# Gate and up projections: two of three matmul passes joined into one, and two sums of weights made by adding transfers

## The chip, the cores and the metric

One core of a Trainium2 chip runs the whole program. The metric is device time in microseconds (us) of one execution, as the median of several. Beside it there is one profiled execution with a trace of every instruction; all durations below are from that one. The engines are PE (matmuls; its weight loads stand apart as PEld), DVE (elementwise work), ACT (copies, casts, activations), POOL and SP. In the part of the program that is changed, SP and POOL only issue transfers (DMA). Each engine works through its own list of instructions in a fixed order, and an instruction that waits holds up all behind it on the same engine.

## The reference

One layer of an encoder on 512 tokens of width 2048, all in float32: a mixer, cross-attention into 256 memory tokens, and a SwiGLU feed-forward part, each between two norms. The change lies in the first half of the feed-forward part, the gate and up projections:

```python
def swiglu_ffn(h, w_gu, w_down):          # h: 512 x 2048, w_gu: 2048 x (5632 gate | 5632 up)
    gate, up = jnp.split(h @ w_gu, 2, axis=-1)
    return (jax.nn.silu(gate) * up) @ w_down
...
x = x + rmsnorm(swiglu_ffn(rmsnorm(x, g[FFN_PRE]), ffn_w_gu[l], ffn_w_down[l]), g[FFN_POST])
```

## The kernel before, in words

The program runs `phase1` (mixer), `phase2` (attention), `gate_up`, `down` and `last`, one after the other. `gate_up` is the stage from about 1440 us to 2330 us of the span.

`gate_up` works through 44 blocks `j` of 128 hidden columns. A block multiplies the 512 tokens by 2048 x 256 weights (128 gate columns and 128 up columns). It is cut into halves three ways: tokens into two halves of 256, the inner dimension into two halves of 1024, columns into gate and up. The 2x2 block product is formed by seven half-size products instead of eight, a scheme of Strassen's kind: each product multiplies a sum of quarters of the activations (`L[1]` to `L[7]`, made once, kept in SBUF) by a sum of quarters of the weights. In the order in which a block runs them, the products are 1, 2, 6, 5, 7, 3, 4. The text calls them P1, P2, P6 and so on.

The four quarters of the weights of a block are `w_gu[j, kh, g]`, 128 x 1024 numbers or 512 KB each: B11 (`kh` 0, gate), B12 (0, up), B21 (1, gate), B22 (1, up). P1, P2 and P3 take B11, B21 and B22 as they are. The other four take sums: S5 = B11 + B12, S6 = S5 + B22, S7 = B12 + B22, S4 = S6 + B21. Before, DVE makes all four (lines 1027, 1030, 1032, 1034 in `right_parts`).

A float32 factor is split into a high and a low part (`split3`): ACT casts the high part (`whi`, line 988), DVE subtracts to get the low part (`wlo`, line 989). A product then runs, for each of 8 inner tiles `k`, three matmuls of 128 weights columns by 256 tokens (`mul3`, lines 177 to 179): high by high, high by low, low by high, all summed into one PSUM bank half. So a product is 24 matmuls and a block of seven is 168. `whi` and `wlo` have three buffers each, so a split can be up to three products ahead of PE.

The first two products of blocks 0 to 4 (`begin`) run early, in the gaps of the end of `phase2`; those blocks then have five products left. Blocks 5 to 43 run all seven.

Results leave PSUM by ACT copies (`f_x`, `f_z`, `f_y`) and DVE operations; three PSUM banks serve a block: `A` for P1, P6, P7 and P4, `B` for P2, `Cc` for P5 and P3. P4 may not start before DVE has read P7 out of bank `A` (line 1142, `f_z`). The block's output `f_h` goes to DRAM by a transfer issued on POOL (line 1155).

Weights come by transfers on SP (line 1114) into tiles named `raw`: those of `kh` 0 into pool `wp` (three buffers), those of `kh` 1 into pool `rp` (three buffers). A transfer into a buffer waits until the last reader of what stood there is done. The order on each engine is not written out by hand: the framework's scheduler sets it from the order of the source and from the pools.

Of the kernel before, what the change touches and what calls it, by code (L numbers as in the profile page):

```python
# [69 lines left out]
def build(tc, x, mem, norm_g, w_in, conv_a_w, pool_w, pool_scale, gdn_conv_w, gdn_A_log,  # L70
# [8 lines left out]
    def pool(name, bufs=1, side=None, stack=None, **kw):  # L79
        return (stack or es).enter_context(tc.tile_pool(name=name, bufs=bufs, side=side, **kw))  # L80
# [814 lines left out]
    def phase2(act):  # L895
        with ExitStack() as s0:
            pp = pool("ptp", stack=s0)
            pt = [tuple(pp.tile([P, 4, T], F32R, name=f"pt{s}{i}") for s in "hl") for i in range(2)]
            with ExitStack() as s1:
                pl = pool("atp", stack=s1)  # L900
                for h in range(XH):
                    qh = pl.tile([P, 4, T], F32R, name="at_qh", bufs=2)
                    ql = pl.tile([P, 4, T], F32R, name="at_ql", bufs=2)
                    proj_a(act, xa_wq, h * XHD, lambda j, o: split(qh[:, j], ql[:, j], o), 2)
                    ks = slice(2 * (h % 2), 2 * (h % 2) + 2)
                    attention(h, qh, ql, pl, pt[h // 2][0][:, ks], pt[h // 2][1][:, ks])
                    if h == 0:
                        value_out(3, pl)
            es_act.close()
            ep = pool("early", 2, "right", es_early)  # L910
            sa12 = pool("sa12", 2, "right", es_a12)
            sa22 = pool("sa22", 2, "right", es_a22)
            stg = pool("stg", 4, "right", es_stg)
            yp = pool("yp2", stack=s0)
            pl2 = pool("adp2", stack=s0)
            xT = [[[p.tile([P, 4, 256], F32, name="stg") for _ in range(2)] for p in q]
                  for q in ((stg, stg), (sa12, sa22))]
            L = {m: [(ep.tile([P, 4, 256], F32R, name=f"L{m}h"), ep.tile([P, 4, 256], F32R, name=f"L{m}l"))
                     for _ in range(2)] for m in (1, 2)}
# [64 lines left out]
    ORDER = (1, 2, 6, 5, 7, 3, 4)  # L984
    FIRST = (5, 6, 7, 4, 3)

    def split3(hl, src):
        nc.scalar.copy(hl[0], src)  # L988
        nc.vector.tensor_tensor(hl[1], src, hl[0].bitcast(F32), op=ALU.subtract)  # L989
# [30 lines left out]
    def right_parts(B11, B12, B21, B22, new, order):  # L1020
# [3 lines left out]
        for m in order:  # L1024
# [9 lines left out]
                tt(s[6], s[6], B21, op=ALU.add)  # L1034
            yield {1: B11, 2: B21, 3: B22, 4: s.get(6), 5: s.get(5), 6: s.get(6), 7: B12}[m]

    def gate_up(xT, L, begun):

        with ExitStack() as s0:
            def factor(name, *ms):  # L1040
                lp = pool(name, 2, stack=s0, reuse_waits="tile")
                for m in ms:
                    L[m] = [(lp.tile([P, 4, 256], F32R, name=f"L{m}h"), lp.tile([P, 4, 256], F32R, name=f"L{m}l"))
                            for _ in range(2)]
            factor("lp", 6, 5, 7)
            tmp = pool("tmpp", 2, stack=s0, reuse_waits="tile")
            parts = [left_parts(xT[0][0][sub], xT[1][0][sub], xT[0][1][sub], xT[1][1][sub],
                                tmp.tile([P, 4, 256], F32, name="tmp"),
                                Lazy(lambda m, sub=sub: L[m][sub]), FIRST) for sub in range(2)]
            rp = pool("rp", 3, stack=s0, reuse_waits="tile")  # L1050
            tp = pool("tp", 2, stack=s0, reuse_waits="tile")
            first = block(0, L, rp, tp, begun[0], FIRST)

            def step():
                for g in parts:
                    next(g)
                next(first)
            step()
            step()
            begun[3] = begin(3, L, tp)  # L1060
            step()
            es_stg.close()
            factor("lp4", 4)
            step()
            begun[4] = begin(4, L, tp)
            es_a22.close()
            factor("lp3", 3)
            step()
            es_a12.close()
            for _ in first:  # L1070
                pass
            for j in range(1, HT):
                for _ in block(j, L, rp, tp, begun.get(j), ORDER[2:]):
                    pass
        es_early.close()

    def product(bank, w, L, m, last=False):
        wh, wl = w
        for k in range(8):
            ah, al = L[m][k // 4]  # L1080
            mul3(bank, wh[:, k], wl[:, k], ah[:, k % 4], al[:, k % 4], k == 0 and m in (1, 2, 5), k == 7, True)

    def split_w(src):
        w = wp.tile([P, 8, P], F32R, name="whi"), wp.tile([P, 8, P], F32R, name="wlo")
# [3 lines left out]
    def begin(j, L, pl):  # L1088


        bank = mm.tile([P, 512], F32, name="mm")
        A, B = bank[:, 0:256], bank[:, 256:512]
        X, g = (pl.tile([P, 256], F32, name="f_" + n, bufs=k) for n, k in (("x", 1), ("g", 3)))
        for m, o, kh in ((2, B, 1), (1, A, 0)):
            b = wp.tile([P, 8, P], F32, name="raw")
            nc.sync.dma_start(b, w_gu[j, kh, 0])
            product(o, split_w(b), L, m)
            if m == 2:
                nc.scalar.copy(X, B)  # L1099
        gate(g, A, X)  # L1100
        return A, g

    def gate(g, o, X):

        nc.vector.tensor_tensor(g, o, X, op=ALU.add)
        nc.scalar.activation(X, g, AF.Tanh, scale=0.5)
        nc.vector.scalar_tensor_tensor(g, X, 1.0, g, op0=ALU.add, op1=ALU.mult)

    def block(j, L, rp, tp, begun, order):

        q = {}
        for kh, g in ((0, 0), (1, 0), (0, 1), (1, 1)):
            q[kh, g] = (rp if kh else wp).tile([P, 8, P], F32, name="raw")
            nc.sync.dma_start(q[kh, g], w_gu[j, kh, g])
        tl = lambda n, bufs=1: tp.tile([P, 256], F32, name="f_" + n, bufs=bufs)
        half = lambda pl, n: pl.tile([P, 512], F32, name=n)[:, 0:256]
        parts = right_parts(q[0, 0], q[0, 1], q[1, 0], q[1, 1], lambda: tp.tile([P, 8, P], F32, name="sum"),
                            (() if begun else (1, 2)) + order)
# [12 lines left out]
        tt, stt = nc.vector.tensor_tensor, nc.vector.scalar_tensor_tensor
        for m in order:
            product(bank[m], split_w(next(parts)), L, m)
            if m == 5:
                Z = tl("z")
                nc.scalar.copy(Z, Cc)
            elif m == 6:
                Y = tl("y")
                nc.scalar.copy(Y, A)
            elif m == 7:  # L1140

                tt(Z, Z, A, op=ALU.subtract)
            elif m == 3:

                tt(Y, Cc, Y, op=ALU.subtract)
                stt(h[:, 0:256], g, 0.5, Y, op0=ALU.mult, op1=ALU.mult)
            else:

                th = tl("t")
                nc.scalar.activation(th, A, AF.Tanh, scale=0.5)  # L1150
                stt(th, th, 1.0, A, op0=ALU.add, op1=ALU.mult)
                stt(h[:, 256:512], th, 0.5, Z, op0=ALU.mult, op1=ALU.mult)
            if m != order[-1]:
                yield
        nc.gpsimd.dma_start(h_d[j], h)
        yield
# [220 lines left out]
```

## Time and profile before

| | us |
|---|---|
| median of 3 runs | 2797.11 (2794.04 to 2797.58) |
| profiled execution, its own time | 2794.72 |
| its span, first to last instruction | 2792.9 |
| PE busy | 2711.8 (97%) |
| DVE busy | 1861.8 (67%) |
| ACT busy | 1222.6 (44%) |
| mean granted clock of PE | 0.989 |

Busy shares are means over stages with different limits. A PE that is busy 97% is not one at its peak, since matmuls overlap in the record; what a matmul costs in a dense stretch is the distance from one start to the next.

### The profile page before, as it was taken

What the parts mean: (1) busy time and instruction counts of PE and PEld (TensorE: products, weight loads), DVE (VectorE), ACT (ScalarE), POOL (GpSimd) and SP (SyncE); (2) the same over time, 40 slices, a digit from 0 to 9 for tenths busy, and PEclk for the clock granted to TensorE, in tenths of its full rate; (3) what the DMA queues carried; (4) which work ended last, traced back from release to release, by engine and by line L of the source; (5) the groups of instructions that cost most, each with busy time, mean ns of one, the idle gap of its engine ahead of it and who ended that gap; (6) DMA issues with size and microseconds to landing.
All of it is one profiled execution on the core that took longest, in us unless ns stands there. A gap on an engine that the chain in (4) does not pass through costs nothing. (4 is left out here: it accounts for less than half of the span.)

```text
span 2792.9 us, 39958 instructions
## 1 busy us (share of the span) xinstructions
PE 2711.8 (97%) x15890; PEld 2385.9 (85%) x15890; DVE 1861.8 (67%) x2693; ACT 1222.6 (44%) x1874; POOL 139.5 (5%) x219
## 2 busy tenths in 40 slices
PE   8999999999999999999979999999999998999997
PEld 6788788878788877888769999999999997888885
DVE  5736557456762364433688787777777778999966
ACT  5623433233552244432544444444444444655542
POOL 0000001100000011000000000000000000000002
PEclk9999999999999999999999999999999999999998
DMA  8733322344675268433544333333333336576656
GB/s 281 243 103 90 88 69 86 106 128 139 213 269 186 98 229 272 163 100 125 185 172 165 120 120 119 114 120 119 118 115 124 110 114 229 196 194 188 173 120 235
DMA packets 158773, 428.38 MB, mean 153 GB/s; under 512 B 18157, under 2 KB 29306, under 8 KB 147706
## 3 DMA queue, kind: packets, MB, share of 16 engines
q1 hardware_dynamic: 140154, 355.57, 38.2%
q0 software_dynamic: 18432, 70.27, 8.6%
q8 instruction: 124, 2.03, 0.3%
q14 instruction: 63, 0.52, 0.1%
HBM read 351.30 MB, written 74.47 MB: 152 GB/s over the span
## 5 line engine op out<-in xcount | busy, mean ns | idle before, releaser
L162 DVE SCALAR_TENSOR_TENSOR wlo<-raw,PA,whi 128x512 fp32r<-128x512 f32 x368 | 263.2, 747 | 297.5 <-ACT whi L161 297.4
L161 ACT ACTIVATE whi<-raw,PA 128x512 fp32r<-128x512 f32 x368 | 247.8, 718 | 396.4 <-PE mm L178 211.2
L177 PE MATMUL mm<-act,whi 128*128 128x512 f32 x832 | 329.8, 396 | 0.0
L179 PE MATMUL mm<-act,wlo 128*128 128x512 f32 x832 | 326.6, 393 | 0.0
L178 PE MATMUL mm<-act,whi 128*128 128x512 f32 x832 | 326.1, 392 | 0.0
L988 ACT CAST whi<-raw 128x1024 fp32r<-128x1024 f32 x176 | 184.6, 1049 | 272.0 <-PE ps L178 133.3
L177 PE MATMUL mm<-whi,act 128*128 128x512 f32 x640 | 252.5, 395 | 3.2 <-ACT act L158 3.0
L178 PE MATMUL mm<-wlo,act 128*128 128x512 f32 x640 | 251.8, 394 | 1.8 <-DVE wlo L162 1.8
L989 DVE TENSOR_TENSOR wlo<-sum,whi 128x1024 fp32r<-128x1024 f32 x132 | 161.4, 1222 | 134.9 <-ACT whi L988 134.7
L179 PE MATMUL mm<-whi,act 128*128 128x512 f32 x640 | 251.0, 393 | 0.2 <-DVE rsq_t L151 0.2
L159 DVE TENSOR_TENSOR wlo<-raw,whi 128x1024 fp32r<-128x1024 f32 x92 | 112.4, 1224 | 192.5 <-ACT whi L158 192.2
L988 ACT CAST whi<-sum 128x1024 fp32r<-128x1024 f32 x132 | 138.3, 1049 | 214.0 <-PE mm L178 129.6
L989 DVE TENSOR_TENSOR wlo<-raw,whi 128x1024 fp32r<-128x1024 f32 x176 | 215.4, 1225 | 19.8 <-ACT whi L988 14.3
L179 PEld LDWEIGHTS mm<-act,wlo 128*128 128x128 f32 x832 | 156.3, 188 | 32.2 <-issue 0.5
L177 PEld LDWEIGHTS mm<-act,whi 128*128 128x128 f32 x832 | 156.4, 188 | 30.8 <-issue 0.7
L178 PEld LDWEIGHTS mm<-act,whi 128*128 128x128 f32 x832 | 156.5, 188 | 30.7 <-issue 0.7
L158 ACT CAST whi<-raw 128x1024 fp32r<-128x1024 f32 x92 | 96.7, 1053 | 188.0 <-PE mm L179 136.7
L177 PEld LDWEIGHTS mm<-whi,act 128*128 128x128 f32 x640 | 121.0, 189 | 30.1 <-ACT act L158 5.1
L178 PEld LDWEIGHTS mm<-wlo,act 128*128 128x128 f32 x640 | 121.0, 189 | 27.5 <-DVE wlo L162 3.0
L179 PEld LDWEIGHTS mm<-whi,act 128*128 128x128 f32 x640 | 120.9, 189 | 25.2 <-DVE act L159 0.6
L988 ACT CAST whB<-rawB 128x1024 fp32r<-128x1024 f32 x80 | 84.1, 1053 | 51.3 <-PE mm L179 50.8
L177 PE MATMUL mm<-L1h,whi 128*128 128x256 f32 x352 | 101.3, 288 | 4.4 <-ACT f_x L1099 4.4
(550 smaller groups left out, 7304.4 us busy)
## 6 DMA issues: line engine op xcount, KB each, us to landing
raw<-in_w_gu_dram SPq DMA_DIRECT2D x186, 512.0 KB, 3.2
raw<-in_w_in_dram SPq DMA_DIRECT2D x88, 512.0 KB, 3.6
rawB<-in_w_down_dram SPq DMA_DIRECT2D x40, 1024.0 KB, 5.4
raw<-in_xa_wkv_dram SPq DMA_DIRECT2D x64, 512.0 KB, 4.5
raw<-in_w_out_dram SPq DMA_DIRECT2D x32, 512.0 KB, 3.7
raw<-in_xa_wo_dram SPq DMA_DIRECT2D x32, 512.0 KB, 6.3
raw<-in_xa_wq_dram SPq DMA_DIRECT2D x32, 512.0 KB, 3.7
raw<-vw_d SPq DMA_DIRECT2D x28, 512.0 KB, 4.1
```

Of the source, the lines that this page charges most:

```text
L158: nc.scalar.copy(hi, src)
L159: nc.vector.tensor_tensor(lo, src, hi.bitcast(F32), op=ALU.subtract)
L161: nc.scalar.activation(hi, src, AF.Copy, scale=scale)
L162: nc.vector.scalar_tensor_tensor(lo, src, scale, hi.bitcast(F32), op0=ALU.mult, op1=ALU.subtract)
L177: nc.tensor.matmul(o, ah, bh, start=start, stop=False, skip_group_check=reopen)
L178: nc.tensor.matmul(o, ah, bl, start=False, stop=False, skip_group_check=reopen)
L179: nc.tensor.matmul(o, al, bh, start=False, stop=stop, skip_group_check=reopen)
L988: nc.scalar.copy(hl[0], src)
L989: nc.vector.tensor_tensor(hl[1], src, hl[0].bitcast(F32), op=ALU.subtract)
```

## The change

Three things change in `gate_up`; nothing outside of it does, apart from line numbers.

1. Each `L[m]` is kept as one tile with the high and the low part side by side (`pair`). For each `k` one matmul of 512 columns multiplies `whi` by both, and a second of 256 columns multiplies `wlo` by the high part. A product is 8 matmuls of 512 and 8 of 256 columns. The bank's second half then holds the high-by-low sum, and has to be added to the first half.
2. For that, the copies and reads out of PSUM take 512 columns in place of 256, and `fold` (a DVE add of 128 x 256) follows on Z, Y and the gate; P4's result is folded with an ACT copy and a DVE add (`f_t2`). `begin` uses one bank for its two products, one after the other.
3. S5 and S7 are no longer made by DVE. SP loads the first quarter into a `raw` tile of pool `wp`, and a second transfer, issued on POOL, adds the other quarter onto it (`accum_op`). S6 and S4 stay on DVE. A block now moves 7 quarters in place of 4 (6 where B11 isn't needed).

```diff
+    def summed_parts(B11, B21, B22, S5, S7, new, order):
+        tt = nc.vector.tensor_tensor
+        t = None
+        for m in order:
+            if m == 6:
+                t = new()
+                tt(t, S5, B22, op=ALU.add)
+            elif m == 4:
+                tt(t, t, B21, op=ALU.add)
+            yield {1: B11, 2: B21, 3: B22, 4: t, 5: S5, 6: t, 7: S7}[m]
...
         for k in range(8):
-            ah, al = L[m][k // 4]
-            mul3(bank, wh[:, k], wl[:, k], ah[:, k % 4], al[:, k % 4], k == 0 and m in (1, 2, 5), k == 7, True)
+            t = L[m][k // 4][:, k % 4]
+            nc.tensor.matmul(bank, wh[:, k], t.rearrange("p s n -> p (s n)"), start=k == 0 and m in (1, 2, 5),
+                             stop=k == 7, **kw)
+            nc.tensor.matmul(bank[:, 0:256], wl[:, k], t[:, 0], start=False, stop=k == 7, **kw)
+
+    def fold(dst, src):
+        nc.vector.tensor_tensor(dst, src[:, 0:256], src[:, 256:512], op=ALU.add)
...
     def gate(g, o, X):
-        nc.vector.tensor_tensor(g, o, X, op=ALU.add)
-        nc.scalar.activation(X, g, AF.Tanh, scale=0.5)
-        nc.vector.scalar_tensor_tensor(g, X, 1.0, g, op0=ALU.add, op1=ALU.mult)
+        nc.vector.tensor_tensor(X, o, X, op=ALU.add)
+        fold(g, X)
+        th = X[:, 0:256]
+        nc.scalar.activation(th, g, AF.Tanh, scale=0.5)
+        nc.vector.scalar_tensor_tensor(g, th, 1.0, g, op0=ALU.add, op1=ALU.mult)
...
+        def load(pl, *halves):
+            b = pl.tile([P, 8, P], F32, name="raw")
+            for i, (kh, g) in enumerate(halves):
+                if i:
+                    nc.gpsimd.dma_start(b, w_gu[j, kh, g], accum_op=ALU.add)
+                else:
+                    nc.sync.dma_start(b, w_gu[j, kh, g])
+            return b
+        B11 = None if begun else load(wp, (0, 0))
+        B21 = load(rp, (1, 0))
+        S5 = load(wp, (0, 0), (0, 1))
+        B22 = load(rp, (1, 1))
+        S7 = load(wp, (0, 1), (1, 1))
...
             elif m == 7:
                 tt(Z, Z, A, op=ALU.subtract)
+                fold(Z[:, 0:256], Z)
             elif m == 3:
                 tt(Y, Cc, Y, op=ALU.subtract)
-                stt(h[:, 0:256], g, 0.5, Y, op0=ALU.mult, op1=ALU.mult)
+                fold(Y[:, 0:256], Y)
+                stt(h[:, 0:256], g, 0.5, Y[:, 0:256], op0=ALU.mult, op1=ALU.mult)
             else:
-                th = tl("t")
-                nc.scalar.activation(th, A, AF.Tanh, scale=0.5)
-                stt(th, th, 1.0, A, op0=ALU.add, op1=ALU.mult)
-                stt(h[:, 256:512], th, 0.5, Z, op0=ALU.mult, op1=ALU.mult)
+                th, g2 = tl("t", 256), tl("t2", 256)
+                nc.scalar.copy(g2, A[:, 256:512])
+                tt(g2, A[:, 0:256], g2, op=ALU.add)
+                nc.scalar.activation(th, g2, AF.Tanh, scale=0.5)
+                stt(th, th, 1.0, g2, op0=ALU.add, op1=ALU.mult)
+                stt(h[:, 256:512], th, 0.5, Z[:, 0:256], op0=ALU.mult, op1=ALU.mult)
```

The order that the scheduler makes of it matters at three places. The first is DVE around the end of a block in the steady part, call it block b. Before, these rows stand from the split of S4 (for P4 of block b) to the split of S6 of the next block. `sum_15612` and `sum_15614` are S5 and S6 of block b+1, made from the `raw` tiles that SP loads; `f_z_15442` is the read of P7 out of bank `A`.

```order
L989 TENSOR_TENSOR wlo_15506<-sum_15382,whi_15505 128x1024
L1030 TENSOR_TENSOR sum_15614<-sum_15612,raw_15544 128x1024
L1142 TENSOR_TENSOR f_z_15442<-f_z_15442,mm_15314 128x256
L989 TENSOR_TENSOR wlo_15551<-raw_15538,whi_15550 128x1024
L1145 TENSOR_TENSOR f_y_15412<-ps_15378,f_y_15412 128x256
L1146 SCALAR_TENSOR_TENSOR f_h_15379<-f_g_15317,f_y_15412 128x256
L989 TENSOR_TENSOR wlo_15580<-raw_15540,whi_15579 128x1024
L989 TENSOR_TENSOR wlo_15617<-sum_15614,whi_15616 128x1024
```

After, the same place on DVE, where `raw_15369` is S5 of block b+1 as the two transfers leave it, `raw_15372` its B22, and `f_z_15289` the read of P7 of block b.

```order
L992 TENSOR_TENSOR wlo_15338<-sum_15245,whi_15337 128x1024
L1047 TENSOR_TENSOR sum_15428<-raw_15369,raw_15372 128x1024
L1175 TENSOR_TENSOR f_z_15289<-f_z_15289,mm_15194 128x512
L992 TENSOR_TENSOR wlo_15382<-raw_15365,whi_15381 128x1024
L1105 TENSOR_TENSOR f_z_15289<-f_z_15289 128x256
L1179 TENSOR_TENSOR f_y_15267<-ps_15243,f_y_15267 128x512
L1105 TENSOR_TENSOR f_y_15267<-f_y_15267 128x256
L992 TENSOR_TENSOR wlo_15403<-raw_15367,whi_15402 128x1024
```

The sum S6 of the next block stands ahead of the read of P7 in both; after, it reads the tile that the adding transfer fills, not one that DVE made itself.

The second place is DVE at the start of a block, after: the rows from the split of S6 of block b+1 on. The last row is the last reader of the S5 tile `raw_15369`, and so what frees its buffer for block b+2.

```order
L992 TENSOR_TENSOR wlo_15431<-sum_15428,whi_15430 128x1024
L1186 TENSOR_TENSOR f_t2_15358<-mm_15194,f_t2_15358 128x256
L1049 TENSOR_TENSOR sum_15428<-sum_15428,raw_15367 128x1024
L1188 SCALAR_TENSOR_TENSOR f_t_15357<-f_t_15357,f_t2_15358 128x256
L1189 SCALAR_TENSOR_TENSOR f_h_15244<-f_t_15357,f_z_15289 128x256
L992 TENSOR_TENSOR wlo_15453<-raw_15369,whi_15452 128x1024
```

Before, the row in the last one's place split a `sum` tile (`wlo_15647<-sum_15612`), for whose buffer no transfer waits, and the sum S5 of the next block followed it; now it reads a `raw` tile that a transfer will fill again. The row of `f_t2` is new.

The third place is POOL. Before, its list in this stage holds one row a block, the output `f_h`. After, it holds three: `raw_15369` and `raw_15374` are the adding transfers for S5 and S7 of block b+1, between the outputs of blocks b-1 (`f_h_15061`) and b (`f_h_15244`).

```order
L1192 DMA h_d_104<-f_h_15061 128x512
L1140 DMA raw_15369<-in_w_gu_dram 128x1024
L1140 DMA raw_15374<-in_w_gu_dram 128x1024
L1192 DMA h_d_104<-f_h_15244 128x512
L1140 DMA raw_15552<-in_w_gu_dram 128x1024
```

An adding transfer stands behind an output that is due in the block before its own. On SP a block's five plain loads now stand in the order B21, B11, B22, first part of S5, first part of S7.

More of the change, by code (lines that the diff above doesn't have):

```diff
@@ L917, in phase2 @@
                   for q in ((stg, stg), (sa12, sa22))]
-            L = {m: [(ep.tile([P, 4, 256], F32R, name=f"L{m}h"), ep.tile([P, 4, 256], F32R, name=f"L{m}l"))
-                     for _ in range(2)] for m in (1, 2)}
+            L = {m: [ep.tile([P, 4, 2, 256], F32R, name=f"L{m}") for _ in range(2)] for m in (1, 2)}
             begun = {}
@@ L926, in f @@
                         for sub in range(2):
-                            split3(L[1][sub], xT[0][0][sub])
-                            split3(L[2][sub], xT[1][0][sub])
+                            split3(pair(L[1][sub]), xT[0][0][sub])
+                            split3(pair(L[2][sub]), xT[1][0][sub])
                     else:
@@ L985, in build, with pair @@
     FIRST = (5, 6, 7, 4, 3)
+    def pair(t):
+        return t[:, :, 0], t[:, :, 1]
     def split3(hl, src):
@@ L1042, in factor @@
                 for m in ms:
-                    L[m] = [(lp.tile([P, 4, 256], F32R, name=f"L{m}h"), lp.tile([P, 4, 256], F32R, name=f"L{m}l"))
-                            for _ in range(2)]
+                    L[m] = [lp.tile([P, 4, 2, 256], F32R, name=f"L{m}") for _ in range(2)]
             factor("lp", 6, 5, 7)
-            tmp = pool("tmpp", 2, stack=s0, reuse_waits="tile")
+            rp = pool("rp", 3, stack=s0, reuse_waits="tile")
+            tp = pool("tp", 2, stack=s0, reuse_waits="tile")
+            es_tmp = ExitStack()
+            tmp = pool("tmpp", 2, stack=es_tmp, reuse_waits="tile")
             parts = [left_parts(xT[0][0][sub], xT[1][0][sub], xT[0][1][sub], xT[1][1][sub],
                                 tmp.tile([P, 4, 256], F32, name="tmp"),
-                                Lazy(lambda m, sub=sub: L[m][sub]), FIRST) for sub in range(2)]
-            rp = pool("rp", 3, stack=s0, reuse_waits="tile")
-            tp = pool("tp", 2, stack=s0, reuse_waits="tile")
+                                Lazy(lambda m, sub=sub: pair(L[m][sub])), FIRST) for sub in range(2)]
             first = block(0, L, rp, tp, begun[0], FIRST)
@@ L1062, in gate_up @@
             es_stg.close()
+            es_tmp.close()
             factor("lp4", 4)
@@ L1075, in gate_up, with product @@
         es_early.close()
-    def product(bank, w, L, m, last=False):
+    def product(bank, w, L, m):
         wh, wl = w
+        kw = dict(skip_group_check=True)
         for k in range(8):
-            ah, al = L[m][k // 4]
-            mul3(bank, wh[:, k], wl[:, k], ah[:, k % 4], al[:, k % 4], k == 0 and m in (1, 2, 5), k == 7, True)
+            t = L[m][k // 4][:, k % 4]
[4 more added lines that the diff above has]
+        nc.vector.tensor_tensor(dst, src[:, 0:256], src[:, 256:512], op=ALU.add)
     def split_w(src):
@@ L1088, in begin @@
     def begin(j, L, pl):
[L1091 to L1094, printed above, removed]
+        A = mm.tile([P, 512], F32, name="mm")
+        X, g = pl.tile([P, T], F32, name="f_x", bufs=1), pl.tile([P, 256], F32, name="f_g", bufs=3)
+        for m, kh in ((2, 1), (1, 0)):
             b = wp.tile([P, 8, P], F32, name="raw")
             nc.sync.dma_start(b, w_gu[j, kh, 0])
-            product(o, split_w(b), L, m)
+            product(A, split_w(b), L, m)
             if m == 2:
-                nc.scalar.copy(X, B)
+                nc.scalar.copy(X, A)
         gate(g, A, X)
@@ L1103, in gate @@
     def gate(g, o, X):
-        nc.vector.tensor_tensor(g, o, X, op=ALU.add)
-        nc.scalar.activation(X, g, AF.Tanh, scale=0.5)
-        nc.vector.scalar_tensor_tensor(g, X, 1.0, g, op0=ALU.add, op1=ALU.mult)
-    def block(j, L, rp, tp, begun, order):
[L1111 to L1118, printed above, removed]
+        nc.vector.tensor_tensor(X, o, X, op=ALU.add)
[3 more added lines that the diff above has]
+        nc.vector.scalar_tensor_tensor(g, th, 1.0, g, op0=ALU.add, op1=ALU.mult)
+    def block(j, L, rp, tp, begun, order):
+        def load(pl, *halves):
[11 more added lines that the diff above has]
+        S7 = load(wp, (0, 1), (1, 1))
+        tl = lambda n, w=T: tp.tile([P, w], F32, name="f_" + n, bufs=1)
+        parts = summed_parts(B11, B21, B22, S5, S7, lambda: tp.tile([P, 8, P], F32, name="sum"),
+                             (() if begun else (1, 2)) + order)
         if begun:
@@ L1121, in block @@
         else:
-            A, B = half(mm, "mm"), half(ps, "ps")
-            X, g = tl("x"), tl("g", 3)
+            A, B = mm.tile([P, 512], F32, name="mm"), ps.tile([P, 512], F32, name="ps")
+            X, g = tl("x"), tp.tile([P, 256], F32, name="f_g", bufs=3)
             product(A, split_w(next(parts)), L, 1)
@@ L1127, in block @@
             gate(g, B, X)
-        Cc = half(ps, "ps")
+        Cc = ps.tile([P, 512], F32, name="ps")
         bank = {6: A, 5: Cc, 7: A, 3: Cc, 4: A}
-        h = tp.tile([P, T], F32, name="f_h", bufs=1)
+        h = tl("h")
         tt, stt = nc.vector.tensor_tensor, nc.vector.scalar_tensor_tensor
```

## The prediction

> **What bounds the kernel now.** I read the page's engine line first, then the tables by stage, then the waits of the stage that is changed, then single instructions there.
>
> ```profile
> PE 2711.8 (97%) x15890; PEld 2385.9 (85%) x15890; DVE 1861.8 (67%) x2693; ACT 1222.6 (44%) x1874; POOL 139.5 (5%) x219
> ```
> ```profile
> 1450.00:1460.00 10.00, 7.49 (x45) 7.08 (x46) 10.00 (x10) 4.43 (x7) 0.00 (x0) 0.83 0.29 104
> 1700.00:1800.00 100.00, 100.00 (x836) 100.00 (x835) 77.67 (x90) 44.04 (x60) 2.70 (x5) 1.00 0.36 119
> 2460.00:2560.00 100.00, 100.00 (x443) 82.84 (x442) 91.10 (x77) 60.85 (x70) 7.74 (x9) 1.00 0.68 187
> ```
>
> Columns of the second fence: stretch, length, then busy time and count of PE, PEld, DVE, ACT, POOL, then granted clock, DMA share, GB/s. In the middle of `gate_up` (second row) PE is never idle and DVE works 78%. Where the stage starts (first row) it is DVE that is full, and PE waits. The third row, from `down`, serves as a model: the same kind of matmul at 512 columns, with adding transfers running.
>
> ```profile
> ACT whi L988 <- PE mm L178: 254.8, 162, 3.6
> DVE wlo L989 <- ACT whi L988: 144.6, 122, 2.0
> SPq L1114 <- DVE sum L1034: 264.5, 39, 7.2
> PE mm L179 <- DVE wlo L989: 0.5, 1, 0.5
> ```
>
> These are waits of the whole stage: total, times, longest. ACT, DVE and SP all wait for work further on; PE waits half a microsecond in 850. So time is won here only by making PE's own list shorter, and lost by whatever makes PE wait.
>
> **What a matmul costs.** The distance of starts counts, not the recorded duration.
>
> ```profile
> 1702.56 0.28 PE L177 MATMUL mm<-L4h,whi 128*128 128x256 f32 x1
> ...
> 1705.43 0.28 PE L177 MATMUL mm<-L1h,whi 128*128 128x256 f32 x1
> ...
> 1810.76 0.54 POOL L1155 DMA_DIRECT2D h_d<-f_h  x1 [19.62 <-DVE f_h L1152]
> 1830.92 0.54 POOL L1155 DMA_DIRECT2D h_d<-f_h  x1 [19.62 <-DVE f_h L1152]
> ```
> ```profile
> 2500.49 0.39 PE L177 MATMUL mm<-whB,B2h 128*128 128x512 f32 x1
> ...
> 2505.93 0.39 PE L177 MATMUL mm<-whB,B6h 128*128 128x512 f32 x1
> ...
> 1412.14 0.39 PE L179 MATMUL mm<-whi,ptl 128*128 128x512 f32 x1
> 1412.36 0.28 PE L177 MATMUL mm<-L2h,whi 128*128 128x256 f32 x1
> 1412.48 0.28 PE L178 MATMUL mm<-L2l,whi 128*128 128x256 f32 x1
> ```
>
> A block of 168 matmuls at 256 columns takes 1830.92 - 1810.76 = 20.16 us, 0.1200 each (24 of them from 1702.56 to 1705.43 say the same). At 512 columns 24 take 5.44 us, 0.2267 each. Doubling the columns costs 0.1067, so 0.0133 us of a matmul is paid whatever its width. A long one followed by short ones (1412.14 on) keeps both prices.
>
> A product now takes 24 x 0.1200 = 2.880 us; after, 8 x (0.2267 + 0.1200) = 2.774. That is 0.106 less, one fixed share per `k`. A block of seven goes from 20.16 to 19.42 us. Blocks 5 to 43 have 39 x 7 and blocks 1 to 4 have 4 x 5 products in the dense part, 293 in all: **31.2 us less**. For the other 15, in the stretch where DVE is full, I count nothing.
>
> The Trainium skill, "TensorE: Matmul & The Clock Gate", section "Back-to-back issue gap", speaks against so much: it puts a warm matmul at N/2.4 ns plus 2.5 ns, so joining two would save 2.5 ns. By that the 31.2 would be an estimated 293 x 8 x 0.0025 = 5.9 us. The rows above disagree, with 13.3 ns.
>
> **The other engines.** Prices:
>
> ```profile
> L988 ACT CAST whi<-raw 128x1024 fp32r<-128x1024 f32 x176 | 184.6, 1049 | 272.0 <-PE ps L178 133.3
> L989 DVE TENSOR_TENSOR wlo<-raw,whi 128x1024 fp32r<-128x1024 f32 x176 | 215.4, 1225 | 19.8 <-ACT whi L988 14.3
> ```
> ```profile
> L1216 ACT COPY eX<-mm x20: 573/587/589, 2345.0 to 2691.1; 128x512 f32<-128x512 f32 x20
> L1254 DVE TENSOR_TENSOR eX<-mm,eX x20: 675/682/692, 2350.3 to 2697.4; 128x512 f32<-128x512 f32 x20
> L1152 DVE SCALAR_TENSOR_TENSOR f_h<-f_t,f_z x44: 414/418/424, 1481.7 to 2331.5; 128x256 f32<-128x256 f32 x44
> ```
> ```profile
> 1808.58 0.41 DVE L1151 SCALAR_TENSOR_TENSOR f_t<-f_t,mm 128x256 f32<-128x256 f32 x1
> 1808.91 1.22 DVE L1034 TENSOR_TENSOR sum<-sum,raw 128x1024 f32<-128x1024 f32 x1
> 1810.05 0.42 DVE L1152 SCALAR_TENSOR_TENSOR f_h<-f_t,f_z 128x256 f32<-128x256 f32 x1
> ...
> 1806.36 1.05 ACT L988 CAST whi<-sum 128x1024 fp32r<-128x1024 f32 x1 [1.88 <-PE mm L178]
> 1807.31 0.38 ACT L1150 ACTIVATE f_t<-mm 128x256 f32<-128x256 f32 x1
> ```
>
> On DVE a block loses two sums (2 x 1.22 = 2.4 us) and gains three reads of PSUM at 512 columns (3 x (0.68 - 0.42) = 0.8), three folds and the add on `f_t2` (4 x 0.42 = 1.7): 2.5. It comes out even, near 15.7 us of 19.4. ACT gains three wider copies and one more, near 1 us, on some 9. Both stay under PE.
>
> At the stage's start, where DVE is the bound, seven wider reads, seven folds and one `f_t2` (7 x 0.69 + 0.42 = 5.2 us) stand against 2.4 for block 0's sums: between 0 and 2.8 us lost, 1.5 taken. At the end, P4's result passes a copy and an add more (0.37 + 0.42) before the next stage's casts, and PE waits for those:
>
> ```profile
> PE mm L177 <- ACT whB L988: 6.9, 1, 6.9
> ```
>
> That is **0.8 us**. So the sum is 31.2 - 1.5 - 0.8 = **28.9 us less**, if the transfers come in time.
>
> **The transfers.** They are the new thing on the path. No adding transfer into SBUF stands in the trace; the nearest are those of `down`, of the same size, from SBUF onto DRAM.
>
> ```profile
> raw<-in_w_gu_dram SPq DMA_DIRECT2D x138, 512.0 KB, 3.2
> ```
> ```profile
> q0 software_dynamic: 4471, 16.28, 32.4%
> ...
> y_d<-eZ POOLq DMA_DIRECT2D x8, 512.0 KB, 5.4
> ...
> y_d<-e POOLq DMA_DIRECT2D x8, 512.0 KB, 6.7
> ```
> ```profile
> y_d<-eZ POOLq DMA_DIRECT2D x2, 512.0 KB, 3.8
> ```
> ```profile
> 1810.19 0.33 SPq L1114 DMA_DIRECT2D raw<-in_w_gu_dram  x1
> ```
>
> The first is the plain load of a quarter: landed 3.2 us after issue. The next fence is `down` from 2425 to 2725 us, all adding: 5.4 us, and 6.7 for the one that falls beside the loads of `hq`. The last but one is the plain store in `down`, 3.8. The price of adding into SBUF thus lies between 3.2 (adding is free) and 6.7; I take 5.4, the row of the same operation beside large loads only. The last row shows SP issuing 0.06 us after the sum at 1808.91 ended.
>
> With three buffers in `wp` and three tiles a block, S5 of block b+1 goes into the buffer of S5 of block b, and its two transfers run one after the other. Time 0 is the start of P1 of block b:
>
> - P1's last matmul starts at 2.65 and is done at 2.93 (0.28). ACT copies `f_x` (0.59, the next may start 0.1 before its end, as at 1807.31), then casts S5: done at 4.5.
> - DVE gets there at about the same time: split of S6 from 1.15 on (P4 of block b-1 freed its buffer at 0), then 1.14 + 0.33 + 1.14 + 0.45 + 0.33 by the distances at 1808.58 to 1810.05. The split of S5 ends at 5.8.
> - SP issues at 5.85, the load lands at 9.05; POOL is free (the output before it is out at about 5.2) and issues; the sum is complete at 14.5.
> - DVE adds S6 of block b+1 from 14.5; 1.14 later, at 15.65, it reads P7 out of bank `A` (0.68), done at 16.35.
> - PE wants bank `A` for P4 at 6 x 2.774 = 16.64.
>
> So there are **0.25 us to spare**, and without them each microsecond of delay stops PE once per block. It holds for S5 of blocks 6 to 43, 38 us per microsecond. The deciding value is the two landings together: 8.6 in this sum, free up to 8.85, and at 9.6 (0.25 + 0.745 more) a block is as long as before. S7 has a buffer from 8 us on and is wanted 17 us later; its cover is wide. The queue on POOL costs nothing, since the output ahead is due long before the load lands.
>
> The 16 engines have room: a plain load takes 31.5% of 700 us over 138, 1.6 us of all of them, from this row of 1600 to 2300 us,
>
> ```profile
> q1 hardware_dynamic: 19872, 72.36, 31.5%
> ```
>
> and an adding one 32.4% of 300 us over 31 (16.28 MB), 3.1 us. A block then needs 5 x 1.6 + 2 x 3.1 = 14.3 of 19.4 us, 74%; `down` runs at 68% and its adding transfers mostly keep to 5.4.
>
> **Rivals.**
>
> 1. *The adding transfer is late and PE stops at P4: slower.* For it: the 6.7 above, and three loads of the next blocks fall in the same 9 us. Against: that 6.7 falls beside loads with short rows, of which `gate_up` has none. At 6.7 the chain is 1.3 later, 1.05 past what is free: 38 x 1.05 = 40 us back, 2808. It is slower from 6.4 on.
> 2. *It is a little late,* 0.3 to 1.0 us by sharing engines: between 2772 and 2797.
> 3. *The fixed share isn't saved:* at 256 columns PEld is busy all the time (100.00 above), so 0.1200 may be the price of a weight load, and a long matmul beside a short one may cost two of them, 0.24. The pair then takes the 0.36 of today's three, only the costs remain, and the time is 2797.1 + 2.3 = 2799, no change. Against it: in `down` PEld has slack (82.84) and the long one costs 0.2267. The Trainium skill's formula, named above, comes out near this case: an estimated 2797.1 - 5.9 + 2.3 = 2793.
> 4. *The short matmul becomes cheaper,* its weights loaded under the long one: at the least 0.1067 for 256 columns, a product of 2.667. Then P4 is due at 16.0, the transfers' 16.3 bind, a block takes 19.0, and the sum is 39 x 1.2 + 20 x 0.21 - 2.3 = 49: about 2749.
>
> **How the numbers follow.** The profiled execution took 2794.7 us; the median of the runs is 2797.1, 2.4 more. 2797.1 - 28.9 = **2768**. Chances: the forecast (2760 to 2776) 0.53; rival 1 0.20; rival 2 0.17; rival 3 0.05; rival 4 0.05. A measurement here can tell 0.2%, 5.6 us, from no change. Faster: 0.53 + 0.05 + 0.12 of rival 2 = 0.70. Same: rival 3 and 0.03 of rival 2 = 0.08. Slower: rival 1 and the last 0.02 = 0.22. The range 2755 to 2808 leaves out the lower part of rival 4 and the worse half of rival 1.
>
> **What would show it.** Right: 1700 to 1800 us holds about 577 matmuls with PE at 100; the rows of `f_h` on POOL stand 19.4 us apart; the adding transfers land in 5 to 5.6 us; DVE waits for the transfer at line 1047 by up to 1 us a block, and PE for `f_z` not at all. Wrong: PE waiting for DVE `f_z` (line 1175) by a steady amount per block (rivals 1, 2), or a distance of two long matmuls other than 0.347 us (rivals 3, 4).

## The result, and the profile after

The changed kernel takes 3010.13 us (median of 4 runs, 3004.59 to 3015.87), against 2795.57 us of the kernel before beside it: a ratio of 1.077, 95% interval 1.0755 to 1.0783. It is slower, and far outside the forecast range. The profiled execution has a span of 3008.2 us, 215.3 more than before.

The outputs of the blocks (`h_d` on POOL) say where. From the start to block 4's output the program lost 6.7 us (1548.68 to 1555.33), from there to block 41's 208.5 us in 37 blocks, in the last two blocks 0.9, and behind them it won 0.7. So it is the steady part, 25.80 us a block where 19.42 was forecast and 20.16 stood before:

```profile
1555.33 0.58 POOL L1192 DMA_DIRECT2D h_d<-f_h  x1 [15.63 <-DVE f_h L1189]
...
2509.77 0.58 POOL L1192 DMA_DIRECT2D h_d<-f_h  x1 [17.31 <-DVE f_h L1189]
```

The engine line, a stretch of 100 us in the table by stage (PE, PEld, DVE, ACT, POOL, granted clock, DMA share, GB/s) and the waits of the stage:

```profile
PE 2773.0 (92%) x13426; PEld 2313.0 (77%) x13426; DVE 1852.3 (62%) x2781; ACT 1266.5 (42%) x1918; POOL 216.0 (7%) x307
```
```profile
1700.00:1800.00 100.00, 86.41 (x448) 74.48 (x448) 61.62 (x80) 38.30 (x52) 9.11 (x12) 0.90 0.59 153
```
```profile
DVE sum L1047 <- DMA raw<-in_w_gu_dram: 210.0, 41, 6.5
...
PE mm L1100 <- DVE f_z L1175: 150.8, 39, 5.1
```

PE has 448 matmuls in 100 us, not 577, and nothing else is full: DVE fell from 78% to 62%. PE waits 39 times, once a block, for `f_z`, the read of P7 out of bank `A`; DVE waits for a transfer just ahead of it. And a new thing: the granted clock is 0.90 where it was 1.00. The transfers from 1560 to 2300 us, with the median from issue to landing:

```profile
raw<-in_w_gu_dram SPq DMA_DIRECT2D x142, 512.0 KB, 4.4
raw<-in_w_gu_dram POOLq DMA_DIRECT2D x58, 512.0 KB, 7.9
```

One block in the timeline, in order of time (start, duration, engine, line; idle time before it and what ended it in brackets):

```profile
2018.23 1.23 DVE L992 TENSOR_TENSOR wlo<-raw,whi 128x1024 fp32r<-128x1024 f32 x1
2019.48 0.33 SPq L1142 DMA_DIRECT2D raw<-in_w_gu_dram  x1
2024.93 0.87 POOL L1140 DMA_DIRECT2D raw<-in_w_gu_dram  x1 [5.81 <-DVE wlo L992]
2026.53 0.87 POOL L1140 DMA_DIRECT2D raw<-in_w_gu_dram  x1 [0.73 <-DMA raw<-in_w_gu_dram]
2030.15 0.28 PE L1102 MATMUL ps<-L,wlo 128*128 128x256 f32 x1
2032.91 1.22 DVE L1047 TENSOR_TENSOR sum<-raw 128x1024 f32<-128x1024 f32 x1 [5.73 <-DMA raw<-in_w_gu_dram]
2034.05 0.68 DVE L1175 TENSOR_TENSOR f_z<-f_z,mm 128x512 f32<-128x512 f32 x1
2034.78 0.79 PE L1100 MATMUL mm<-L,whi 128*128 128x512 f32 x1 [4.35 <-DVE f_z L1175]
...
2040.07 0.63 PE L1100 MATMUL mm<-L,whi 128*128 128x512 f32 x1
2040.71 0.51 PE L1100 MATMUL mm<-L,whi 128*128 128x512 f32 x1
2041.17 0.40 PE L1100 MATMUL mm<-L,whi 128*128 128x512 f32 x1
```

That is rival 1's place and mechanism. The split of S5 ends at 2019.46, SP issues the base load at 2019.48, POOL the adding one 5.45 us later, and DVE gets the sum 7.98 us behind that: 13.4 us where the forecast had 8.6 and 8.85 was free. P3's last matmul starts at 2030.15; P4 starts 4.6 us later. Then it runs at half speed:

```profile
2033.00:2034.00 1.00, 0.00 (x0) 0.00 (x0) 1.00 (x1) 0.00 (x0) 0.00 (x0) 1.00 0.79 156
2034.00:2035.00 1.00, 0.22 (x1) 0.22 (x2) 1.00 (x3) 0.00 (x0) 0.00 (x0) 0.55 0.28 53
...
2039.00:2040.00 1.00, 1.00 (x4) 0.80 (x4) 0.00 (x0) 0.00 (x0) 0.00 (x0) 0.50 0.00 0
...
2041.00:2042.00 1.00, 1.00 (x7) 0.87 (x7) 0.78 (x1) 0.45 (x2) 0.00 (x0) 1.00 0.03 8
```

In this block the clock falls to 0.50 some 4 us after PE stopped and is back 6 us after PE has started again. So a stop has two prices: the stop, and the slow matmuls after it.

### The profile page after: what moved, and what is told of

It reads as the page before. It is cut to its first block, busy times and chain, and to the rows that moved or that the text cites. A ratio compares the mean times of both kernels' runs of the same rounds, so it can differ in the third digit from the quotient of the medians.

```text
span 3008.2 us, 35590 instructions
## 1 busy us (share of the span) xinstructions
PE 2773.0 (92%) x13426; PEld 2313.0 (77%) x13426; DVE 1852.3 (62%) x2781; ACT 1266.5 (42%) x1918; POOL 216.0 (7%) x307
## 5 line engine op out<-in xcount | busy, mean ns | idle before, releaser
L1100 PE MATMUL mm<-L,whi 128*128 128x512 f32 x1448 | 597.9, 446 | 159.8 <-DVE f_z L1175 152.1
L1100 PEld LDWEIGHTS mm<-L,whi 128*128 128x128 f32 x1448 | 312.8, 216 | 250.5 <-DVE f_z L1175 164.8
L1102 PE MATMUL mm<-L,wlo 128*128 128x256 f32 x1448 | 440.8, 305 | 3.3 <-DVE wlo L992 3.3
L1100 PE MATMUL ps<-L,whi 128*128 128x512 f32 x1016 | 360.8, 395 | 5.6 <-DVE L L992 5.6
L1102 PEld LDWEIGHTS mm<-L,wlo 128*128 128x128 f32 x1448 | 314.9, 217 | 4.8 <-DVE wlo L992 4.4
L1102 PE MATMUL ps<-L,wlo 128*128 128x256 f32 x1016 | 284.0, 280 | 0.0
L1100 PEld LDWEIGHTS ps<-L,whi 128*128 128x128 f32 x1016 | 190.5, 188 | 50.0 <-issue 5.8
L992 DVE TENSOR_TENSOR wlo<-sum,whi 128x1024 fp32r<-128x1024 f32 x88 | 107.7, 1224 | 139.7 <-ACT whi L991 139.4
L1102 PEld LDWEIGHTS ps<-L,wlo 128*128 128x128 f32 x1016 | 191.7, 189 | 0.0
L1047 DVE TENSOR_TENSOR sum<-raw 128x1024 f32<-128x1024 f32 x44 | 53.9, 1224 | 210.0 <-DMA raw<-in_w_gu_dram 210.0
```

The costliest lines, as they stand in the source:

```text
L1047: tt(t, S5, B22, op=ALU.add)
L1100: nc.tensor.matmul(bank, wh[:, k], t.rearrange("p s n -> p (s n)"), start=k == 0 and m in (1, 2, 5), stop=k == 7, **kw)
L1102: nc.tensor.matmul(bank[:, 0:256], wl[:, k], t[:, 0], start=False, stop=k == 7, **kw)
```

## The experiments

Theory A: the joined matmul saves what was forecast; the two transfers into S5's buffer are late, the read of P7 stands behind the sum that needs them in DVE's list, PE stops, and its clock falls. The rivals were that the joined matmul is dear (B), that the traffic as such is too much (C), and variants on the adding transfer itself (D, E). The column "block" is the mean of 37 blocks between the outputs of blocks 4 and 41 in the profiled execution.

| kernel | median us | ratio to before, interval | block, us |
|---|---|---|---|
| changed kernel | 3010.1 | 1.0769, 1.0755 to 1.0783 | 25.80 |
| e1, sums on DVE | 2778.4 | 0.9939, 0.9917 to 0.9960 | 19.39 |
| e6, old matmuls | 3013.6 | 1.0771, 1.0712 to 1.0830 | 25.16 |
| e3, two S5 buffers | 2791.3 | 0.9977, 0.9959 to 0.9995 | 19.43 |
| e4, no add | 2896.3 | 1.0370, 1.0346 to 1.0394 | 22.91 |
| e7, sum later | 2782.9 | 0.9935, 0.9910 to 0.9960 | 19.43 |
| e8, filled stop | 2947.8 | 1.0546, 1.0529 to 1.0562 | 23.84 |
| e5, S5 alone by adding | 3015.2 | 1.0784, 1.0767 to 1.0800 | 25.79 |
| e2, S7 alone by adding | 2784.7 | 0.9937, 0.9911 to 0.9962 | 19.79 |
| e11, fewer loads | 2829.6 | 1.0119, 1.0103 to 1.0134 | 20.85 |
| e9, e7 grouped | 2773.1 | 0.9915, 0.9901 to 0.9929 | 19.55 |
| e10, e2 grouped | 2777.0 | 0.9927, 0.9914 to 0.9939 | 19.55 |
| e12, e1 grouped | 2771.3 | 0.9909, 0.9894 to 0.9924 | 19.55 |

**Each part alone.** e1 keeps parts 1 and 2 of the change:

```diff
-        B21 = load(rp, (1, 0))
-        S5 = load(wp, (0, 0), (0, 1))
...
+        B11, B21, B12, B22 = load(wp, (0, 0)), load(rp, (1, 0)), load(wp, (0, 1)), load(rp, (1, 1))
...
-        parts = summed_parts(B11, B21, B22, S5, S7, lambda: ...
+        parts = right_parts(B11, B12, B21, B22, lambda: ...
```

> Parts 1 and 2 of the change alone: one matmul for two passes, all four sums of weights on DVE again, four plain loads a block. Theory A (the loss comes from the two transfers into the buffer of S5, one after the other: PE stops at P4 of each block for about 4.5 us, and its clock is low for about 2.5 us more): both go, the joined matmul keeps its 0.106 us a product, and the time is 2768 (2762 to 2778; DVE then has 18 of 19.4 us a block). Theory B (the joined matmul costs as much as the three it replaces or more): 2797 or more.

e6 is the kernel before with `summed_parts` and the adding transfers alone.

> Part 3 alone: the sums S5 and S7 by adding transfers, the three matmuls of before. Theory A: the transfers take as long as in the changed kernel, P4 is due 0.6 us later (6 x 2.88 = 17.28 us), so PE stops about 3.7 us a block and runs about 2.5 us more at a low clock: 38 x 6.2 = 236 us more than before, near 3030 (2990 to 3045). Theory B: the adding transfers cost nothing, near 2797.

The same stretch by stage, first e1, then e6 with a wait of 1560 to 2300 us:

```profile
1700.00:1800.00 100.00, 100.00 (x579) 87.45 (x578) 89.53 (x113) 50.34 (x67) 2.69 (x5) 1.00 0.39 123
```
```profile
1700.00:1800.00 100.00, 81.45 (x608) 80.64 (x607) 46.35 (x56) 32.31 (x44) 8.53 (x11) 0.88 0.57 152
```
```profile
PE mm L177 <- DVE f_z L1163: 100.2, 30, 5.4
```

e1 has PE full, 579 matmuls (577 were forecast), a block of 19.39 us and a profiled execution of 2767.6. Its runs spread from 2767.6 to 2784.8, which the last group of experiments takes up. e6 has the loss with the old matmuls, 219 us where theory A had 236, and the low clock too; its profiled execution, 2985.0, is the fastest of its four, so 25.16 us a block is less than its median would have. Theory B falls: the loss is in the transfers.

**Where the chain can be cut.** e3 gives S5 a pool of its own, e7 moves the sum that waits for it (`lo[-1]` is the newest split, that for P2 of the sum's own block); neither takes a transfer away.

```diff
+            sp = pool("sp", 2, stack=s0, reuse_waits="tile")
             for j in range(1, HT):
...
-        S5 = load(wp, (0, 0), (0, 1))
+        S5 = load(sp or wp, (0, 0), (0, 1))
```

> The changed kernel with S5 in two buffers of its own from block 1 on, so that its first transfer needn't wait for the split of the S5 before it; the same seven transfers a block and the same adding. Theory A (buffer chain): S5 is complete long before it is wanted, PE doesn't stop, and the time is that of the prediction, 2768 to 2778. Theory C (seven transfers a block with two adding ones take too much of the transfer engines, whatever they wait for): it stays near 3010, at least above 2900.

```diff
-                tt(t, S5, B22, op=ALU.add)
+                s6 = tt(t, S5, B22, op=ALU.add)
+                tc.add_manual_dep(s6.ins, lo[-1].ins.name, ..., reason="order")
...
```

> The changed kernel, the same seven transfers, buffers and adds; only DVE's list is altered: the sum S6 of block b+1 stands behind the split for its P2, so the read of P7 of block b is no longer queued behind the adding transfer. Theory A (PE stops because the read stands behind the late S5 in DVE's list, not because S5 itself is wanted then): the chain still ends 19 to 20 us after the start of block b, but S6 is wanted by P6 at 24.97, so its sum may start as late as 21.5: no stop, 2768 to 2785. Rival (the transfers are late by themselves, and the stop moves from P4 to P6): 2850 or more.

First e3, its stretch and its transfers, then the same of e7, and one of its waits:

```profile
1700.00:1800.00 100.00, 100.00 (x578) 87.42 (x578) 79.60 (x104) 50.60 (x67) 11.40 (x15) 1.00 0.75 211
```
```profile
raw<-in_w_gu_dram POOLq DMA_DIRECT2D x74, 512.0 KB, 5.5
```
```profile
1700.00:1800.00 100.00, 100.00 (x579) 88.19 (x578) 79.44 (x104) 51.73 (x69) 11.40 (x15) 1.00 0.74 199
```
```profile
raw<-in_w_gu_dram SPq DMA_DIRECT2D x183, 512.0 KB, 4.7
raw<-in_w_gu_dram POOLq DMA_DIRECT2D x74, 512.0 KB, 7.6
```
```profile
DVE sum L1047 <- DMA raw<-in_w_gu_dram: 8.2, 14, 1.0
```

Both are at 19.43 us a block with all seven transfers, so theory C falls: the engines carry 211 GB/s at a share of 0.75. e7 is the sharper one. Its adding transfers take nearly as long as in the changed kernel (7.6 against 7.9), and it costs nothing: S5 lands 3.5 to 6.3 us after the read of P7 has begun, in all 37 blocks of 1560 to 2300 us, and was not wanted yet. What stopped PE was the read of P7 queued behind a sum that could have waited. e3's median is above its forecast, and higher than its steady part explains: in its profile 24.2 us lie between the outputs of blocks 0 and 1, against 14.9 in e1. Its new pool opens only where earlier ones are closed; that this is the cause was not tried.

**What makes the second transfer late.** e4 lets it overwrite and not add, e5 drops the one for S7, e11 drops the loads of B21 and B22.

```diff
-                    nc.gpsimd.dma_start(b, w_gu[j, kh, g], accum_op=ALU.add)
+                    nc.gpsimd.dma_start(b, w_gu[j, kh, g])
```

> The changed kernel with the second transfer of S5 and S7 overwriting and not adding (so S5 and S7 are the second quarter alone). The waits, the buffers, the queues and the bytes read stay. Theory A with the add as the long part: the second transfer takes 4.4 us like the first one, not 8.0, so the two take 4.9 + 0.5 + 4.4 = 9.8 against the 8.85 that are free: a stop of about 1 us a block, too short for the clock to fall, 2768 + 38 = about 2806 (2770 to 2820). Theory C' (it is the second transfer's place on POOL's queue behind the plain loads that costs, not the adding): 8 us again and about 3010.

```diff
-        S7 = load(wp, (0, 1), (1, 1))
+        S7 = load(wp, (0, 1))
...
+            elif m == 7:
+                tt(S7, S7, B22, op=ALU.add)
```

> The changed kernel with S7 made by DVE again from a plain load; S5 alone by two transfers. Theory A (the add of S5 takes 8.0 us because the add of S7 is issued 1.6 us behind it, and 5.5 when it runs alone): the chain ends 5.8 + 0.05 + 4.4 + 0.5 + 5.5 = 16.25, the read of P7 is done at 18.1 against 16.64: a stop of 1.5 us, with up to 1.6 us for the clock, 2768 + 38 x (1.5 to 3.1) = 2825 to 2886. Rival (an adding transfer takes 8 us here by itself): 3000.

```diff
-        B21 = load(rp, (1, 0))
+        B21, B22 = kept or (load(rp, (1, 0)), None)
...
-        B22 = load(rp, (1, 1))
+        if not kept:
+            B22 = load(rp, (1, 1))
...
```

> The changed kernel without the plain loads of B21 and B22 from block 5 on: those of block 4 are used again (S4, S6, P2 and P3 work on old numbers). S5 and S7 still come by two transfers each, with the same buffers and the same order. Theory D (the adding transfer of S5 takes 7.6 to 8 us because it stands behind the plain loads that SP issues beside it, up to two in 4 us; the add itself is 5.5, as where the queue is empty): the base lands in 3.6, the add in 5.5 to 6.5, the read of P7 is done at 5.85 + 3.6 + 0.5 + 6 + 1.85 = 17.8 against 16.64, a stop near 1 us with or without 1.6 for the clock, 2768 + 38 x (0.5 to 2.5) = 2787 to 2863. Theory E (an adding transfer takes 8 us in this place whatever stands before it): read done at 19.8, a stop of 3.2 and 1.9 for the clock, 2768 + 38 x 5.1 = 2960.

POOL's transfers of 1560 to 2300 us in e4, e5 and e11, and e11's on SP:

```profile
raw<-in_w_gu_dram POOLq DMA_DIRECT2D x64, 512.0 KB, 5.5
```
```profile
raw<-in_w_gu_dram POOLq DMA_DIRECT2D x29, 512.0 KB, 7.6
```
```profile
raw<-in_w_gu_dram SPq DMA_DIRECT2D x106, 512.0 KB, 3.6
raw<-in_w_gu_dram POOLq DMA_DIRECT2D x70, 512.0 KB, 5.8
```

In e4 the add is worth 7.9 - 5.5 = 2.4 us. But a block still takes 22.91, and my 2806 was 90 us too low. PE stops for 2 us there, and in the block shown that is enough to bring the clock down (rows of PE, then of the table by stage):

```profile
2036.68 0.50 PE L1100 MATMUL mm<-L,whi 128*128 128x512 f32 x1 [2.05 <-DVE f_z L1175]
```
```profile
2036.00:2037.00 1.00, 0.32 (x1) 0.30 (x2) 1.00 (x3) 0.00 (x0) 0.00 (x0) 1.00 0.00 0
...
2038.00:2039.00 1.00, 1.00 (x4) 0.80 (x4) 0.97 (x3) 0.00 (x0) 0.00 (x0) 0.50 0.26 49
```

The clock fell so behind 19 of e4's 38 stops; the shortest of the 19 lasted 1.76 us, the longest of the others 2.79.

e5 went against me: S5's add takes 7.6 us with no add for S7 near it, and the block is as long as in the changed kernel. What stands ahead of it shows in the transfer engines. In e5 SP issues a plain load at the same moment as POOL the add; here the two issues, and the queues' shares from 2004.4 to 2007.5 and from 2007.5 to 2010.9:

```profile
2004.36 0.87 POOL L1142 DMA_DIRECT2D raw<-in_w_gu_dram  x1 [5.49 <-DMA raw<-in_w_gu_dram]
```
```profile
2004.40 0.33 SPq L1144 DMA_DIRECT2D raw<-in_w_gu_dram  x1
```
```profile
q1 hardware_dynamic: 151, 0.55, 66.8%
```
```profile
q0 software_dynamic: 136, 0.51, 82.2%
q1 hardware_dynamic: 54, 0.16, 13.5%
```

In the first of these stretches only plain packets (q1) move; in the second the add (q0) has most of the engines. Its first packet starts 3.46 us after the issue. In e3 the add of S7, issued at the row below, meets empty queues; its first packet starts after 1.56 us, and from 2006 to 2009.3 us its packets fill the engines:

```profile
2004.69 0.85 POOL L1141 DMA_DIRECT2D raw<-in_w_gu_dram  x1 [8.61 <-DMA raw<-in_w_gu_dram]
```
```profile
q0 software_dynamic: 131, 0.52, 92.0%
```

So an add is 1.6 us to the first packet and about 3 us of all engines, 5.3 to its landing there, and waits for plain loads already under way. e3 holds both kinds side by side: from 1560 to 2300 us S5's adds, most of them issued at the same moment as a plain load, take 6.8 us in the median, S7's 5.25, and the 5.5 above is the median of all. e11 puts it to the test: with two plain loads fewer a block, the base lands in 3.6 and the add in 5.8 with the add of S7 still behind it, a block is 20.85, and 2829.6 lies in theory D's range. Theory E falls.

**What the clock costs.** e8 puts 16 matmuls into the stop:

```diff
+            if m == 4 and not begun:
+                D = mm.tile([P, 512], F32, name="mm")
+                t = L[1][0].rearrange("p a s n -> p (a s n)")
+                ds = [nc.tensor.matmul(D, wt[0][:, k % 8], t[:, 0:512], ...) for k in range(16)]
```

> The changed kernel with 16 matmuls of 512 columns (16 x 0.2267 = 3.6 us) put into PE's list ahead of P4 in blocks 5 to 43; their result goes to a bank that nobody reads. They fill most of the 4.5 us in which PE stands still. Theory A with the clock (the granted clock is 0.50 for 6 us behind each stop, and that costs 2.5 us a block): the clock stays up, a block takes 24 instead of 26.45 us, about 2915, though PE does more work. Rival (the matmuls of P4 are slow for another reason, such as the transfers): no change, 3010, or more by what doesn't fit into the stop.

```profile
1700.00:1800.00 100.00, 98.93 (x537) 84.14 (x537) 62.02 (x81) 40.99 (x54) 9.65 (x13) 1.00 0.66 167
```
```profile
raw<-in_w_gu_dram POOLq DMA_DIRECT2D x62, 512.0 KB, 8.0
```

With as slow transfers (8.0) and more work it is 62 us faster, at a clock of 1.00. I had forecast 95. A block takes 23.84 us: 56 pairs at 0.353 (19.78), 16 x 0.2267 = 3.63 of filling, 0.43 left of the stop. So PE is held up for 4.06 us (the waits in the changed kernel's own trace, 150.8 us in 39, are 3.87 each), and of the 25.80 of the changed kernel 25.80 - 19.41 - 4.06 = 2.33 us are the clock, about as forecast (2.5). The difference from 95 is that the whole stage was not as bad as the one block that the forecast went by (26.45), and that the pair is slower here (0.353), which is the next point.

**Two rhythms of a pair, and a grouped version.** e2 leaves S5 on DVE and adds B22 onto B12's buffer once DVE has read it:

```diff
                 tt(s[5], B11, B12, op=ALU.add)
+                if B22_d is not None:
+                    nc.gpsimd.dma_start(B12, B22_d, accum_op=ALU.add)
...
```

> The changed kernel with S5 made by DVE again and S7 alone by an adding transfer, onto the quarter B12 after DVE has read it for S5; five transfers a block. Theory A (S7's cover is wide, S5's chain is the whole loss): no stop, 2768 to 2780, one sum less on DVE than with four sums there. Rival (any adding transfer in this stage makes something late): over 2800.

```profile
1700.00:1800.00 100.00, 100.00 (x568) 86.77 (x567) 83.85 (x108) 49.78 (x66) 7.12 (x10) 1.00 0.49 145
```
```profile
raw<-in_w_gu_dram POOLq DMA_DIRECT2D x37, 512.0 KB, 5.4
```

S7's cover is wide, as forecast: PE never waits. Yet the median, 2784.7, lies 5 us above the forecast range, and PE, full and at a clock of 1.00, does 568 matmuls where e1 and e7 do 579: a pair of long and short takes 0.353 us in this execution, all through the stage, and 0.347 in those. The executions of e1, e2 and e7 go with it: but for one at 2774, they lie at 2767 to 2771 or at 2782 to 2786.

The kernels with stops show where the two come from. Cut at the stops, and without the time at half clock, e4, e11 and the changed kernel have 96 stretches from 1560 to 2300 us, and in 95 of them the pairs keep one of the two distances from the restart of PE to the next stop: 45 at 0.347, 50 at 0.353, mixed within each of the three executions. So the rhythm changes at a restart and otherwise stays. Where nothing stops PE, one start would decide 39 blocks: 39 x 0.37 = 14.4 us, about the distance of the two groups. What makes a restart take the one or the other is open.

So I put the 8 long matmuls of a product ahead of its 8 short ones:

```diff
         for k in range(8):
             t = L[m][k // 4][:, k % 4]
             nc.tensor.matmul(bank, wh[:, k], t.rearrange("p s n -> p (s n)"), ...)
+        for k in range(8):
+            t = L[m][k // 4][:, k % 4]
             nc.tensor.matmul(bank[:, 0:256], wl[:, k], t[:, 0], ...)
```

> The changed kernel with S6's sum later in DVE's list, and each product's 8 long matmuls first, then its 8 short ones. So far the executions of the kernels without a stop come in two groups, near 2767 and near 2784, and the two profiles that show them have a long and a short matmul 0.347 and 0.353 us apart from the next pair all through the stage. Theory F (the 0.006 us arises at the change from short to long and back): one change in place of eight, all executions near 2767 (a block of 19.4 us). Rival (it belongs to the short matmul or to the execution): two groups again, 2767 and 2784.

> The kernel with S7 alone by an adding transfer, and each product's 8 long matmuls first, then its 8 short ones. Theory F: all executions near 2767 to 2770. Rival: two groups again, near 2767 and 2784. With five in place of seven transfers a block, the fewer of the two versions.

> The joined matmul with all four sums on DVE and no adding transfer, and each product's 8 long matmuls first, then its 8 short ones. Theory F: all executions near 2768. Rival: two groups again, 2768 and 2784. The short matmuls come 1.8 us later than before, which gives DVE's split that much more time, so DVE at 90% shouldn't hold PE up.

The stretch of e12:

```profile
1700.00:1800.00 100.00, 100.00 (x575) 88.01 (x575) 89.98 (x114) 49.48 (x66) 3.24 (x6) 1.00 0.41 125
```

All three profiles have 19.55 us a block, and the 13 executions lie between 2768 and 2779. Theory F holds for the two groups, which are gone, but not for the place: the one that is left lies between them. The grouped kernels ran on another chip (9) than e1 (2), e2 and e7 (4), and no alternating kernel without a stop ran beside them, so that the grouping and not the chip ended the two groups is likely, and not shown. e12, with no adding transfer at all, has the lowest median, 2771.3 us, 0.9% under the kernel before; its interval overlaps those of e1, e2, e7, e9 and e10, so which of them is best is not settled.

## Why the prediction was wrong

- **The joined matmul: right.** Eight pairs at 0.2267 + 0.1200 gave 19.42 us a block and 577 matmuls in 100 us; e1 and e7 have 19.39 and 19.43, and 579. Their profiled executions, 2767.6 and 2767.4, are the 2768 of the forecast. Rivals 3 and 4 fall. What the forecast did not have is the second rhythm, 0.37 us a block: most of their executions lie in the slower group, so that in the medians e1 is 15.9 and e7 14.1 us under the kernel before, half of the 28.9.
- **The transfers: the step that failed.** The place was right to the instruction, the size was not. The base load was put at 3.2 us and took 4.4 (median of all plain loads), POOL's reaction at nothing and took 0.56, the add at 5.4 and took 7.9. Together that is 12.9 in the median and 13.4 in the block shown, against 8.85 that were free. POOL's reaction alone is more than the 0.25 us that were left to spare. The 5.4 holds here too where no plain load is ahead (e2: 5.4; S7 in e3: 5.25). In the changed kernel the event that frees S5's buffer comes among the loads of the next block, so the base load shares the engines and the add stands behind the loads. I took the mean load (74%; e3 shows 0.75) for what the engines have at that moment. The other price was in the profile before: the 6.7 that the forecast put down to short rows is the median of eight adding transfers in `down`, four of 5.1 to 5.4 us and four of 7.9 to 9.1. From 1.5 to 5 us after the issue, plain packets took 56 to 83% of the engines in the slow four and at most 7.4% in the others. Two of the eight, issued at 2534.21 and 2649.18 us:

```profile
y_d<-e POOLq DMA_DIRECT2D x1, 512.0 KB, 5.4
y_d<-e POOLq DMA_DIRECT2D x1, 512.0 KB, 9.1
```

- **The price of a stop: also failed.** Rival 1 was counted at 1 us for 1 us, 2808 at a landing of 6.7. Each stop also costs 2.33 us of half clock. With 4.06 + 2.33 = 6.39 us, which is what a block measured above 19.41, in each of the 38 blocks, 2768 becomes 2768 + 243 = 3011; measured 3010. The Trainium skill, "TensorE: Matmul & The Clock Gate", section "Part 1: The HAM clock gate", says that the clock falls to half after an idle window of about 3.4 us and comes back after as long a busy one. The trace agrees on the half (0.50) and on 3.4 us as the step: behind 37 stops of the changed kernel the clock is low for 3.41 us (16 times) or 6.83 (21 times), and these stretches begin whole multiples of 3.41 us apart. It does not agree on the idle time, which can be shorter: 1.76 us were enough once in e4.
- **That nothing else is late: right.** S7's cover, POOL's queue and the mean of the engines' share cost nothing (e2, e3, e7). The start is open: up to block 4's output the forecast comes to 0.6 us won (1.5 lost, 20 products at 0.106 won); the changed kernel lost 6.7, e1 lost 2.8 and e7 won 0.7, and the causes of this spread were not traced. Behind the last block 0.7 us were won where 0.8 lost was forecast.
- **The dependence I took for given.** I named the buffer as the reason for the chain and accepted the order on DVE as fixed. For P6 the sum of the next block may start at 21.5 us, for P4 it had to start at 14.8 (16.64 - 1.85); e7 shows that only its place ahead of the read of P7 made it urgent.

## What to carry to other kernels

A transfer's latency has to be read from rows in which the same neighbours are under way, and it must be asked what else the same event releases: here a buffer's release started a load, and the adding transfer behind it met the loads of the next block. If a late arrival is waited for on an in-order engine, look at what stands behind that wait; moving one sum by a few places was worth all that a second set of buffers was worth. And a stop of PE of four microseconds a block is not priced by its length, since the slow clock after it cost more than half as much again (2.33 on 4.06 us).

## What the runs showed of the hardware

- An adding transfer of 512 KB into SBUF lands in 5.3 to 5.4 us when no plain load is ahead of it (medians of S7 in e3 and e2) and in 6.8 to 8.0 beside plain loads (S5 in e3; both adds in e8); an overwriting one from the same queue took 5.5 beside loads (e4), and a plain one from SP 3.2 (before) to 5.2 (e2).
- Issued at the same moment as a plain load, an adding transfer started its first packet 3.46 us after the issue (e5); with empty queues it took 1.56 us (e3).
- Behind PE's stops the granted clock went to 0.50 for 3.41 or 6.83 us: after 37 stops of 2.55 to 5.09 us in the changed kernel, after 19 of 38 in e4 (0.43 to 3.87 us) and after 3 of 36 in e11 (29.1 us in 35 waits from 1560 to 2300 us, 0.8 each).
- A long and a short matmul in turn take 0.347 or 0.353 us at the same granted clock, and keep the one or the other from a restart of PE to its next stop; eight of each in a row take 2.793 together in e9, e10 and e12.
